# A hybrid convolution / state-space layer on one core: low weight parts from adding transfers, queues and products reassigned

## The chip, the core and the metric

The kernel runs on one core of a Trainium2 chip. Five engines work side by side, each through its own instructions in order: TensorE (PE: matrix products), VectorE (DVE), ScalarE (ACT), GpSimd (POOL) and SyncE (SP). They meet through semaphores. The scratch memory has 128 partitions; matrix products end in PSUM. The metric is the device time of one execution in microseconds, the median of several.

## The reference

One layer over 512 latent tokens (width 1024) with a context of 256 tokens ahead of them, in float32. Cut to what matters:

```python
h  = modulate(rmsnorm(x, norm1_w), mod[0], mod[1])       # hc likewise, from ctx
proj = h @ w_in                                          # columns: x, B, C, dt, z, glu, gate
glu = proj[..., COL_GLU:COL_GATE]
u = glu[..., :CONV_DIM] * sigmoid(glu[..., CONV_DIM:])
u = dwconv(u, conv_dw_w, conv_dw_b)                      # 31 taps along rows of 64
u_conv = silu(layernorm(u)) @ w_conv_out + b_conv_out
xs, bm, cm, dt_f, dt_b = ssd_inputs(proj, lp)            # 5 taps and SiLU on x, B, C
y_f, _ = ssd_scan(xs, dt_f, a[0], bm, cm, h_f)           # chunks of 128, both directions,
y_b, _ = ssd_scan(flip(xs), flip(dt_b), a[1], flip(bm), flip(cm), h_b)   # from context states
y = y_f + flip(y_b) + ssd_d * xs
u_ssd = rmsnorm(y * silu(z), ssm_norm_w) @ w_ssm_out
x = x + mod[2] * ((g_conv * u_conv + g_ssd * u_ssd) @ w_o)   # g: sigmoid of the gate columns
x = x + mod[5] * sq_relu_mlp(modulate(rmsnorm(x, norm2_w), mod[3], mod[4]), w_mlp1, w_mlp2)
out = rmsnorm(x, final_norm_w)
```

There are 8 groups of 4 heads; each has its own B and C (128 columns each), two tiles of x (X0, X1) and two of z (Z0, Z1).

## The kernel before

All activations lie transposed: a tile is 128 channels by 512 tokens. A matrix product in nearly full float32 is made from halves: a value v is split into a high part that TensorE takes (`whi`, `hh`) and a low part, the rest (`wlo`, `hl`). `gemm` runs, for each of 8 slices k of the 1024 inputs, high·high (L118), high·low (L119) and low·high (L120), 24 matmuls into one PSUM tile `ps`; 24 more of 256 columns follow where the context is needed (B, X0, X1).

`load_w` brings one weight of 128 output columns: SP starts the transfer of 512 KB into `raw` (L100, three buffers), ACT casts it to `whi` (L109), DVE subtracts, `wlo = raw - whi` (L110). `whi` and `wlo` have two buffers each, so the weight after next can be split only when the matmuls of a weight are through with its buffer.

Each group g has two stages. `proj(g)` runs B, C, X0, X1, Z0, Z1 through `gemm`; `taps5` evicts the PSUM tile on ACT with the middle tap (L377) and adds four taps on DVE straight from PSUM (L381), after which ACT applies SiLU (L391). `ssd(g)` makes the scan: C·B products `cps`, evicted to `cb`; transposes of B into `bps`, evicted by ACT to `Bk` (L485); transposes of X into `xps`; states `sps`; and for j = 0, 1 the output `yps`, with the decays. For these, rows that hold one head's values over time are broadcast from memory to all partitions: `E` rows (started by SP, L459; masked by POOL's affine_select, L463; exponentials on ACT, L466), and `Cd` rows (started by SP, L537; multiplied by C, L538: three of four on POOL, that of direction 0 and r = 1 on DVE). `yt` is then scaled and gated on DVE, stored to `s_y` by SP (L560), squared on ACT (L565) and added to `yacc` on POOL.

Behind the groups 0 to 4 a GLU tile is run: two more weights through `gemm` and 31 taps on DVE (`conv`, L593), the result added to `cacc` on POOL (L598). Three GLU tiles, the gates, the two branch projections, `w_o` and the MLP follow; there, too, `load_w` and `gemm` run all weights.

The program is written stage after stage, but a scheduler sets the order on each engine by priorities: `later(n)` moves what stands in it n places later (or earlier, if negative). Weights are asked for 300 places early, evictions 400. So matmuls of `proj(g + 1)` stand between those of `ssd(g)`, and an engine's row of instructions mixes both.

Of the kernel before, what the change touches and what calls it, by code (L numbers as in the profile page):

```python
# [8 lines left out]
F32 = mybir.dt.float32  # L9
F32R = mybir.dt.float32r  # L10
BF16 = mybir.dt.bfloat16
AF = mybir.ActivationFunctionType
ALU = mybir.AluOpType

P = 128
D = 1024
KT = 8
T = 512
# [32 lines left out]

WARM = 22

DECAYS_V = ((0, 1),)

W_EARLY, EVICT, EVICT_GLU, EVICT_FIRST = 300, 400, 200, 0
GLU_LATER, TAPS_LATER, LATE_LATER = 90, 650, 300
DT_LATER, LN_LATER, ROWS_LATER, BEGIN_LATER = 200, 100, 60, 60
# [2 lines left out]
def build(tc, xT, ctxT, cond, crow, wada1, wada2, vecs, hv, cst, w_in, w_co, w_so, w_o, w_1, w_2, outT):  # L61
    nc = tc.nc
    with ExitStack() as es:
# [26 lines left out]
        @contextmanager  # L90
        def later(n):

            tc.cur_priority += n
            yield
            tc.cur_priority -= n


        def load_raw(src):
            raw = wp.tile([P, KT, P], F32, name="raw", tag="raw", bufs=3)
            nc.sync.dma_start(raw, src)  # L100
            return raw

        def load_w(src, hi=None, lo=None, early=W_EARLY):
            with later(-early):
                raw = load_raw(src)
                if hi is None:
                    hi = wp.tile([P, KT, P], F32R, name="whi", tag="whi")
                    lo = wp.tile([P, KT, P], F32R, name="wlo", tag="wlo")
                nc.scalar.copy(hi, raw)  # L109
                nc.vector.tensor_tensor(lo, raw, hi, ALU.subtract)  # L110
            return hi, lo

        def gemm(ps, w, rhs, start=True, stop=True, t0=0, t1=None, k0=0, k1=KT):
            whi, wlo = w
            rhi, rlo = rhs
            ps = ps[:, t0:t1]
            for k in range(k0, k1):
                nc.tensor.matmul(ps, lhsT=whi[:, k, :], rhs=rhi[:, k, t0:t1], start=start and k == 0, stop=False)  # L118
                nc.tensor.matmul(ps, lhsT=whi[:, k, :], rhs=rlo[:, k, t0:t1], start=False, stop=False)  # L119
                nc.tensor.matmul(ps, lhsT=wlo[:, k, :], rhs=rhi[:, k, t0:t1], start=False, stop=stop and k == KT - 1)  # L120

        psum_pools = [pp]
        turn = [0]

# [72 lines left out]
        with tc.tile_pool(name="st", bufs=1) as st:  # L197
# [43 lines left out]
            for i in range(4):  # L241
# [12 lines left out]
                ps = pm.tile([P, T], F32, name="aps", tag="pm")  # L254
                for k in range(KT):
                    for j in range(4):
                        nc.tensor.matmul(
                            ps[32 * j:32 * j + 32, 0:P], lhsT=sc[:, k, :], rhs=blk[:, k, j * P:(j + 1) * P],
                            start=k == 0, stop=k == KT - 1)
# [35 lines left out]
        s_y = dr.tile([2 * KT, P, T], F32, name="s_y")  # L295
# [73 lines left out]
        spool = inner.enter_context(tc.tile_pool(name="sp", bufs=2))  # L369
# [49 lines left out]
        yacc = acct("yacc")  # L419
# [3 lines left out]
        never = nc.gpsimd.to_reg(NEVER)  # L423

        def proj(g):
            s = W_GRP + 6 * g
            if g == 0:
                _, Bt, Ct, X = first_xbc
            else:
                Bt = xbc(s, 16 + g, True, "Bt")  # L430
                Ct = xbc(s + 1, 24 + g, False, "Ct")
                X = [xbc(s + 2 + j, 2 * g + j, True, "Xt") for j in range(2)]
            Z = []
            for j in range(2):
                w = load_w(w_in[s + 4 + j], early=W_EARLY if g else 0)
                ps = ps_big()
                gemm(ps, w, rh)
                z = tp.tile([P, T], F32, name="Z", tag="Z", bufs=2)
                with later(-EVICT):
                    nc.scalar.activation(z, ps, AF.Silu)  # L440
                Z.append(z)
            return Bt, Ct, X, Z
# [28 lines left out]
        def ssd(g, Bt, Ct, X, Z):  # L471
# [19 lines left out]
            for c0 in (4, 0, 2):  # L491
# [10 lines left out]
                for d in range(2):  # L502
                    lo = c0 + 1 if (d == 1 and c0 == 0) else c0
                    hi = c0 + 1 if (d == 0 and c0 == 2) else c0 + 2
# [17 lines left out]
            for s in range(NCH - 1):  # L522
                ps = states(((s,), (3 - s,)))
# [6 lines left out]
            for j in range(2):  # L530
                yps = py.tile([P, T], F32, name="yps", tag="py")
                Ms, Cs = [], ([], [])
                for r in range(2):
                    for d in range(2):
                        hd = d * HEADS + 4 * g + 2 * j + r
                        Cd = (spool if d else tp).tile([P, T], F32, name="Cd", tag="Cd", bufs=CDB if d else 3)
                        nc.sync.dma_start(Cd, s_cf[hd, 1].unsqueeze(0).broadcast_to([P, T]))  # L537
                        (nc.vector if (d, r) in DECAYS_V else nc.gpsimd).tensor_tensor(Cd, Ct, Cd, ALU.mult)  # L538
                        Cs[d].append(Cd)
                    M = ahead.pop(0)  # L540
                    nc.vector.tensor_tensor(M, M, cb, ALU.mult)
                    Ms.append(M)
                expo(4 * g + 2 * j + 2 + LEAD)
                for k in range(3):
                    for c in range(NCH):
                        for r in range(2):
                            o = yps[64 * r:64 * r + 64, c * P:(c + 1) * P]
                            hr = 2 * j + r
                            if k == 2:
                                nc.tensor.matmul(o, lhsT=xt[:, c, hr, :], rhs=ch(Ms[r], c),  # L550
                                                 start=False, stop=True, skip_group_check=True)
# [5 lines left out]
                yt = tp.tile([P, T], F32, name="yt", tag="yt", bufs=2)  # L557
                nc.vector.scalar_tensor_tensor(yt, X[j][:, :T], vcol(V_D + t), yps, ALU.mult, ALU.add)
                nc.vector.tensor_tensor(yt, yt, Z[j], ALU.mult)
                nc.sync.dma_start(s_y[t], yt)  # L560
                if t == 0:
                    nc.scalar.activation(yacc, yt, AF.Square)
                else:
                    q = spool.tile([P, T], F32, name="ysq", tag="ysq", bufs=1)
                    nc.scalar.activation(q, yt, AF.Square)  # L565
                    nc.gpsimd.tensor_tensor(yacc, yacc, q, ALU.add)


# [35 lines left out]
        for g in range(G):  # L604
# [3 lines left out]
            if g in GLU_AT:  # L608
                with later(GLU_LATER):
                    q = glu(GLU_AT.index(g), spool, "sg")  # L610
                with later(TAPS_LATER):
                    taps(*q)
        late = list(range(len(GLU_AT), KT))
        inner.close()
        b2 = es.enter_context(tc.tile_pool(name="b2", bufs=5))
        p2 = es.enter_context(tc.tile_pool(name="p2", bufs=4, space=bass.MemoryType.PSUM))
# [278 lines left out]
```

## Time and profile before

| | |
|---|---|
| time, median of 3 runs | 1246.62 us (1246.41 to 1251.65) |
| profiled execution | 1245.49 us, its span 1243.7 us |
| granted TensorE clock, mean | 0.991 |
| busy: PE / DVE / ACT / POOL | 1203.5 / 922.5 / 549.8 / 167.7 us |
| transfers | 169.83 MB, mean 137 GB/s |

In the span the groups with their GLU tiles lie at about 110 to 503 us, some 70 us each, groups 6 and 7 to about 600, the late GLU tiles, gates and projections to about 900, the MLP behind them. The page's waits name an instruction that waited, the engine and line that released it, and the idle time. Matmuls overlap: a busy time of 0.39 us at a distance of 0.23 from start to start is full pace, and a gap is seen in the distance of starts.

### The profile page before, as it was taken

The page shows a single profiled execution, that of the slowest core. Times are in us where ns is not written, and L with a number is a line of the kernel's source. Part 1 is how long each engine was busy: PE and PEld are TensorE (multiplying, and loading weights), DVE is VectorE, ACT ScalarE, POOL GpSimd, SP SyncE. Part 2 cuts the span into 40 slices and gives each one's busy share as a digit, 9 for nine tenths or more (in the row PEclk, how much of TensorE's full clock was granted, in tenths as well). Part 3 has the DMA queues.
Part 4 walks back from the last instruction along what each step waited for, and adds up shares of the span by engine and source line. Part 5 has one row for each costly group of instructions (what it writes and reads, how often), then busy time and mean ns, then how long its engine had stood idle before and what let it go on. Part 6 is the DMA issues. An engine that isn't in the chain of part 4 may idle for free.

```text
span 1243.7 us, 17422 instructions
## 1 busy us (share of the span) xinstructions
PE 1203.5 (97%) x6662; PEld 995.1 (80%) x6662; DVE 922.5 (74%) x1426; ACT 549.8 (44%) x904; POOL 167.7 (13%) x138
## 2 busy tenths in 40 slices
PE   7999999999999999999999999999999999999997
PEld 3787888787777787787888788789988888888886
DVE  6799799898998989776999698777733343443454
ACT  4557976454554446342453461234422332322342
POOL 0004623141332423120010000000000000000000
PEclk7999999999999999999999999999999999999998
DMA  9427762533534352422353468855112332333322
GB/s 368 158 62 209 232 203 85 153 103 111 161 107 165 110 161 77 136 70 92 121 185 116 130 195 289 311 164 183 35 48 88 102 95 91 103 92 95 102 85 68
DMA packets 65331, 169.83 MB, mean 137 GB/s; under 512 B 7648, under 2 KB 10464, under 8 KB 65120
## 3 DMA queue, kind: packets, MB, share of 16 engines
q1 hardware_dynamic: 65248, 168.72, 42.6%
q8 instruction: 52, 0.85, 0.3%
q14 instruction: 31, 0.25, 0.1%
HBM read 162.14 MB, written 6.55 MB: 136 GB/s over the span
## 4 chain that ended last, share of the span: by engine, by line
PE 60%; DVE 19%; DMA 9%; ACT 6%; issue 3%; SPq 1%; POOL 1%; DVEq 0%; ACTq 0%; POOLq 0%
PE ps L118 18%; PE ps L120 18%; PE ps L119 18%; DVE conv L593 5%; DMA E<-s_cf 4%; DVE wlo L110 3%; DVE Xt L381 3%; ACT E L466 2%; PE sps L515 2%; DMA aw<-in_wada_dram 2%; DMA Cd<-s_cf 1%; PE yps L554 1%; ACT whi L109 1%; DVE Ct L381 1%; DVE Cd L538 1%
## 5 line engine op out<-in xcount | busy, mean ns | idle before, releaser
L109 ACT CAST whi<-raw 128x1024 fp32r<-128x1024 f32 x163 | 170.9, 1049 | 360.5 <-PE ps L119 329.0
L110 DVE TENSOR_TENSOR wlo<-raw,whi 128x1024 fp32r<-128x1024 f32 x163 | 202.3, 1241 | 94.7 <-ACT whi L109 86.6
L118 PE MATMUL ps<-hh,whi 128*128 128x512 f32 x632 | 255.7, 405 | 5.1 <-DVE Xt L381 2.4
L120 PE MATMUL ps<-hh,wlo 128*128 128x512 f32 x632 | 254.5, 403 | 5.5 <-DVE wlo L110 5.5
L119 PE MATMUL ps<-hl,whi 128*128 128x512 f32 x632 | 253.5, 401 | 0.0
L593 DVE SCALAR_TENSOR_TENSOR conv<-sg,V,conv 128x392 f32<-128x392 f32 (+14 forms) x240 | 181.6, 774 | 1.7
L120 PEld LDWEIGHTS ps<-hh,wlo 128*128 128x128 f32 x632 | 118.9, 188 | 35.2 <-DVE wlo L110 9.5
L118 PEld LDWEIGHTS ps<-hh,whi 128*128 128x128 f32 x632 | 118.8, 188 | 34.4 <-issue 9.7
L119 PEld LDWEIGHTS ps<-hl,whi 128*128 128x128 f32 x632 | 118.8, 188 | 24.8 <-issue 1.3
L730 DVE SCALAR_TENSOR_TENSOR x<-ps,mod,x 128x512 f32<-128x512 f32 (+1 forms) x48 | 31.6, 661 | 99.1 <-PE ps L120 99.1
L466 ACT ACTIVATE E<-E,bT 128x128 f32<-128x128 f32 x256 | 79.7, 394 | 38.9 <-POOL E L463 38.8
L120 PE MATMUL ps<-h2h,wlo 128*128 128x512 f32 (+1 forms) x240 | 89.9, 376 | 0.0
L119 PE MATMUL ps<-h2l,whi 128*128 128x512 f32 (+1 forms) x240 | 89.7, 375 | 0.0
L118 PE MATMUL ps<-h2h,whi 128*128 128x512 f32 (+1 forms) x240 | 89.7, 376 | 0.0
L119 PE MATMUL ps<-gl,whi 128*128 128x512 f32 x224 | 88.4, 395 | 0.0
L118 PE MATMUL ps<-gh,whi 128*128 128x512 f32 x224 | 88.2, 394 | 0.0
L120 PE MATMUL ps<-gh,wlo 128*128 128x512 f32 x224 | 87.9, 392 | 0.0
L538 POOL TENSOR_TENSOR Cd<-Ct,Cd 128x512 f32<-128x512 f32 x48 | 77.0, 1636 | 64.7 <-ACT Ct L391 56.1
L463 POOL TENSOR_SCALAR_AFFINE_SELECT E<-E 128x512 f32<-128x512 f32 x64 | 55.4, 878 | 207.7 <-DMA E<-s_cf 188.8
L381 DVE SCALAR_TENSOR_TENSOR Xt<-ps,V,Xt 128x510 f32<-128x510 f32 (+3 forms) x128 | 74.9, 607 | 2.6 <-ACT Xt L377 2.1
L118 PE MATMUL ps<-hc,whi 128*128 128x256 f32 x184 | 52.2, 284 | 1.4 <-DVE Xt L381 1.4
L119 PE MATMUL ps<-hc,whi 128*128 128x256 f32 x184 | 52.3, 284 | 0.0
(260 smaller groups left out, 2286.4 us busy)
## 6 DMA issues: line engine op xcount, KB each, us to landing
raw<-in_w_in_dram SPq DMA_DIRECT2D x81, 512.0 KB, 3.6
raw<-in_w_dram SPq DMA_DIRECT2D x64, 512.0 KB, 3.7
E<-s_cf SPq DMA_DIRECT2D x64, 256.0 KB, 4.6
Cd<-s_cf SPq DMA_DIRECT2D x64, 256.0 KB, 5.1
aw<-in_wada_dram SPq DMA_DIRECT2D x64, 256.0 KB, 4.3
ablk<-in_wada_dram SPq DMA_DIRECT2D x16, 512.0 KB, 8.3
raw<-in_w_so_dram SPq DMA_DIRECT2D x16, 512.0 KB, 3.7
s_y<-yt SPq DMA_DIRECT2D x16, 256.0 KB, 3.2
```

Of the source, the lines that this page charges most:

```text
L109: nc.scalar.copy(hi, raw)
L110: nc.vector.tensor_tensor(lo, raw, hi, ALU.subtract)
L118: nc.tensor.matmul(ps, lhsT=whi[:, k, :], rhs=rhi[:, k, t0:t1], start=start and k == 0, stop=False)
L119: nc.tensor.matmul(ps, lhsT=whi[:, k, :], rhs=rlo[:, k, t0:t1], start=False, stop=False)
L120: nc.tensor.matmul(ps, lhsT=wlo[:, k, :], rhs=rhi[:, k, t0:t1], start=False, stop=stop and k == KT - 1)
L381: nc.vector.scalar_tensor_tensor(o[:, lo:hi], ps[:, lo + d:hi + d], vcol(V_SCW + 5 * ch + j), o[:, lo:hi], ALU.mult, ALU.add)
L463: nc.gpsimd.affine_select(x3, x3, pattern=[[0, NCH], [sign, P]], compare_op=ALU.is_ge, fill=never, base=0, channel_multiplier=-sign)
L466: nc.scalar.activation(x3[:, c], x3[:, c], AF.Exp, bias=bT[:, c, hd:hd + 1])
L515: nc.tensor.matmul(ps[:, d * 256:(d + 1) * 256], lhsT=ch(Bk, c), rhs=xw[d][:, wi[d](c)].rearrange("p h e -> p (h e)"), start=i == 0, stop= ...
L538: (nc.vector if (d, r) in DECAYS_V else nc.gpsimd).tensor_tensor(Cd, Ct, Cd, ALU.mult)
L593: nc.vector.scalar_tensor_tensor(o[:, :, lo:hi], u[:, :, lo + d:hi + d], wv(j), o[:, :, lo:hi], ALU.mult, ALU.add)
L730: nc.vector.scalar_tensor_tensor(x1[:, j, a:b], ps[:, a:b], mod[:, gcol + j, 0:1], x1[:, j, a:b], ALU.mult, ALU.add)
```

## The change

From `proj(2)` on, until the pools of the groups are closed, `by_dma` is set: for the 36 weights of `proj(2)` to `proj(7)` and the 8 of the GLU tiles behind groups 1 to 4. There ACT starts the transfer of `raw` in place of SP. ACT casts `whi` as before and then writes `-raw` into `wlo`, which in that tile's type is minus the high part; POOL then starts a transfer of the same 512 KB from memory that adds to `wlo`, so that the low part is left. DVE subtracts nothing for these weights. All 64 products of C's rows are made by DVE. The square of `yt` goes to ACT first and the store to `s_y` is started by ACT behind it, so that SP starts only rows there. In the whole kernel `gemm` runs, where it covers all eight slices, the 16 matmuls with `whi` first and the 8 with `wlo` behind them.

```diff
-DECAYS_V = ((0, 1),)
-
         def load_raw(src):
             raw = wp.tile([P, KT, P], F32, name="raw", tag="raw", bufs=3)
-            nc.sync.dma_start(raw, src)
+            (nc.scalar if by_dma[0] else nc.sync).dma_start(raw, src)
             return raw
 
         def load_w(src, hi=None, lo=None, early=W_EARLY):
+            kept = hi is not None
             with later(-early):
...
                 nc.scalar.copy(hi, raw)
-                nc.vector.tensor_tensor(lo, raw, hi, ALU.subtract)
+                if kept or not by_dma[0]:
+                    nc.vector.tensor_tensor(lo, raw, hi, ALU.subtract)
+                else:
+
+                    nc.scalar.activation(lo, raw, AF.Copy, scale=-1.0)
+                    nc.gpsimd.dma_start(lo, src, accum_op=ALU.add)
             return hi, lo
 
         def gemm(ps, w, rhs, start=True, stop=True, t0=0, t1=None, k0=0, k1=KT):
...
+            whole = k0 == 0 and k1 == KT
+
+            def with_lo(k):
+                nc.tensor.matmul(ps, lhsT=wlo[:, k, :], rhs=rhi[:, k, t0:t1], start=False, stop=stop and k == KT - 1)
+
             for k in range(k0, k1):
                 nc.tensor.matmul(ps, lhsT=whi[:, k, :], rhs=rhi[:, k, t0:t1], start=start and k == 0, stop=False)
                 nc.tensor.matmul(ps, lhsT=whi[:, k, :], rhs=rlo[:, k, t0:t1], start=False, stop=False)
-                nc.tensor.matmul(ps, lhsT=wlo[:, k, :], rhs=rhi[:, k, t0:t1], start=False, stop=stop and k == KT - 1)
-
+                if not whole:
+                    with_lo(k)
+            if whole:
+                for k in range(KT):
+                    with_lo(k)
...
         def proj(g):
+            by_dma[0] = g > 1
...
                         nc.sync.dma_start(Cd, s_cf[hd, 1].unsqueeze(0).broadcast_to([P, T]))
-                        (nc.vector if (d, r) in DECAYS_V else nc.gpsimd).tensor_tensor(Cd, Ct, Cd, ALU.mult)
+                        nc.vector.tensor_tensor(Cd, Ct, Cd, ALU.mult)
...
-                nc.sync.dma_start(s_y[t], yt)
-                if t == 0:
-                    nc.scalar.activation(yacc, yt, AF.Square)
-                else:
-                    q = spool.tile([P, T], F32, name="ysq", tag="ysq", bufs=1)
-                    nc.scalar.activation(q, yt, AF.Square)
+                q = spool.tile([P, T], F32, name="ysq", tag="ysq", bufs=1) if t else yacc
+                nc.scalar.activation(q, yt, AF.Square)
+                nc.scalar.dma_start(s_y[t], yt)
+                if t:
                     nc.gpsimd.tensor_tensor(yacc, yacc, q, ALU.add)
...
         late = list(range(len(GLU_AT), KT))
+        by_dma[0] = False
         inner.close()
```

How this moves instructions is shown at three places of `proj(3)` and `ssd(2)`. Line numbers differ: the evictions L377 stand on L391 in the changed kernel, the exponentials L466 on L481, the masks L463 on L478, Bk L485 on L500, cacc L598 on L611, the cast L109 on L108; L98 is the start of a raw weight, L113 the negated copy, L114 the adding transfer.

ACT around X0's weight, before: `Bt` is B's eviction (512 columns of latents, 256 of context), `E` the exponentials, `Ct` C's eviction.

```order
L377 ACTIVATE Bt_2426<-ps_2427,V_72 128x512
L466 ACTIVATE E_2982<-E_2982,bT_575 128x128 x2
L109 CAST whi_2528<-raw_2526 128x1024
L377 ACTIVATE Bt_2426<-ps_2457,V_72 128x256
L466 ACTIVATE E_2982<-E_2982,bT_575 128x128 x2
L466 ACTIVATE E_2997<-E_2997,bT_575 128x128 x4
L466 ACTIVATE E_3529<-E_3529,bT_575 128x128 x4
L466 ACTIVATE E_3536<-E_3536,bT_575 128x128 x4
L377 ACTIVATE Ct_2494<-ps_2495,V_72 128x512
```

The same place after the change:

```order
L391 ACTIVATE Bt_2435<-ps_2436,V_72 128x512
L481 ACTIVATE E_2998<-E_2998,bT_575 128x128 x3
L481 ACTIVATE E_3005<-E_3005,bT_575 128x128
L108 CAST whi_2538<-raw_2536 128x1024
L391 ACTIVATE Bt_2435<-ps_2466,V_72 128x256
L113 ACTIVATE wlo_2539<-raw_2536 128x1024
L481 ACTIVATE E_3005<-E_3005,bT_575 128x128
L98 DMA raw_2708<-in_w_in_dram 128x1024
L481 ACTIVATE E_3005<-E_3005,bT_575 128x128
L108 CAST whi_2607<-raw_2605 128x1024
L481 ACTIVATE E_3005<-E_3005,bT_575 128x128
L481 ACTIVATE E_3013<-E_3013,bT_575 128x128 x2
```

X0's negated copy stands behind the eviction of B's context part, a transfer of a later weight and X1's cast among the exponentials.

ACT at the start of the next scan, before: `cb` and `Bk` are the evictions that `ssd` begins with.

```order
L478 COPY cb_2830<-cps_2825 128x512
L466 ACT_TABLE_LOAD
L466 ACTIVATE E_3551<-E_3551,bT_575 128x128
L485 COPY Bk_2832<-bps_2833 128x512
L485 COPY Bk_2832<-bps_2839 128x256
```

And after it:

```order
L493 COPY cb_2846<-cps_2841 128x512
L98 DMA raw_3167<-in_w_in_dram 128x1024
L500 COPY Bk_2848<-bps_2849 128x512
L500 COPY Bk_2848<-bps_2855 128x256
L481 ACT_TABLE_LOAD
L481 ACTIVATE E_3020<-E_3020,bT_575 128x128
```

The table load and the exponential went behind the two copies, and the start of a transfer came ahead of them.

POOL over the same stretch, before: the products of C (`Cd`), the masks of rows (`E`) and the two adds.

```order
L538 TENSOR_TENSOR Cd_2978<-Ct_2494,Cd_2978 128x512
L463 AFFINE_SELECT E_3551<-E_3551 128x512
L463 AFFINE_SELECT E_3612<-E_3612 128x512
L463 AFFINE_SELECT E_3627<-E_3627 128x512
L598 TENSOR_TENSOR cacc_585<-cacc_585,conv_720 128x512
```

And after it, from X0's weight on:

```order
L478 AFFINE_SELECT E_3553<-E_3553 128x512
L478 AFFINE_SELECT E_3560<-E_3560 128x512
L114 DMA wlo_2539<-in_w_in_dram 128x1024
L114 DMA wlo_2608<-in_w_in_dram 128x1024
L478 AFFINE_SELECT E_3575<-E_3575 128x512
L114 DMA wlo_2677<-in_w_in_dram 128x1024
L114 DMA wlo_2711<-in_w_in_dram 128x1024
L114 DMA wlo_2745<-in_w_in_dram 128x1024
L611 TENSOR_TENSOR cacc_585<-cacc_585,conv_720 128x512
L114 DMA wlo_2779<-in_w_in_dram 128x1024
```

Where the products of C were, POOL starts the adding transfers of X0, X1, Z0, Z1 and of the GLU tile's two weights, the last behind the add to `cacc`.

More of the change, by code (lines that the diff above doesn't have):

```diff
@@ L119, in gemm @@
                 nc.tensor.matmul(ps, lhsT=whi[:, k, :], rhs=rlo[:, k, t0:t1], start=False, stop=False)
-                nc.tensor.matmul(ps, lhsT=wlo[:, k, :], rhs=rhi[:, k, t0:t1], start=False, stop=stop and k == KT - 1)
+                if not whole:
[3 more added lines that the diff above has]
+                    with_lo(k)
+        by_dma = [False]
         psum_pools = [pp]
```

## The prediction, made before the changed kernel was run

> **What bounds the kernel now.** I read the page's busy times first, then windows cut at the group periods, then PE's waits inside them, then the timelines around each wait.
>
> ```profile
> PE 1203.5 (97%) x6662; PEld 995.1 (80%) x6662; DVE 922.5 (74%) x1426; ACT 549.8 (44%) x904; POOL 167.7 (13%) x138
> 293.30:364.20 70.90, 67.39 (x407) 55.73 (x408) 65.79 (x94) 34.12 (x66) 22.15 (x18) 1.00 0.42 129
> 950.00:1000.00 50.00, 50.00 (x221) 41.11 (x220) 20.51 (x23) 15.68 (x20) 0.00 (x0) 1.00 0.32 95
> ```
>
> A window row gives start:end and length, then busy time of PE, PEld, DVE, ACT and POOL, clock, DMA share, GB/s. PE is the bound: in 950:1000 it never rests, and 50.00 / 221 = 0.226 us is the pace of a 512-column matmul. The clock is full, so only gaps between matmuls can be won. In a period of a group with a GLU tile (such as 293.3:364.2) DVE is nearly as full as PE, and there the gaps lie:
>
> ```profile
> PE ps L120 <- DVE wlo L110: 5.1, 7, 0.7
> PE yps L554 <- DVE Cd L538: 3.3, 5, 0.9
> PE ps L118 <- DVE Xt L381: 2.4, 4, 0.7
> PE xps L495 <- ACT Bk L485: 1.5, 4, 0.4
> PE ps L118 <- DVE Bt L381: 0.4, 2, 0.2
> ```
>
> These are PE's waits in 222.7:560.7 (us in all, times, longest). One of them in PE's timeline (start, us, at the end the idle time):
>
> ```profile
> 327.93 0.40 PE L119 MATMUL ps<-hl,whi 128*128 128x512 f32 x1
> 329.05 0.50 PE L120 MATMUL ps<-hh,wlo 128*128 128x512 f32 x1 [0.73 <-DVE wlo L110]
> 329.39 0.40 PE L118 MATMUL ps<-hh,whi 128*128 128x512 f32 x1
> 329.63 0.39 PE L119 MATMUL ps<-hl,whi 128*128 128x512 f32 x1
> ```
>
> From 327.93 to 329.63 stand three steps, 0.68 us at the pace; they took 1.70. The wait shown as 0.73 cost 1.0, so a stall costs its idle time and some 0.27 us. The low part was late in DVE's queue, behind taps:
>
> ```profile
> 326.34 1.53 DVE L381 SCALAR_TENSOR_TENSOR Bt<-ps,V,Bt 128x254 f32<-128x254 f32 x3 [0.40 <-ACT Bt L377]
> 327.79 1.21 DVE L110 TENSOR_TENSOR wlo<-raw,whi 128x1024 fp32r<-128x1024 f32 x1
> ```
>
> **What is won.** The subtract leaves DVE for 44 weights: the 36 of proj(2) to proj(7) and the 8 of four GLU tiles. With 0.27 for each wait: low parts 5.1 + 7×0.27 = 7.0; Xt (a PSUM buffer that DVE's taps release late) 2.4 + 4×0.27 = 3.5; Bt 0.4 + 2×0.27 = 0.9. Bk is late on ACT:
>
> ```profile
> 361.38 1.28 ACT L466 ACT_TABLE_LOAD   x1 [1.05 <-DMA E<-s_cf]
> 363.22 0.40 ACT L466 ACTIVATE E<-E,bT 128x128 f32<-128x128 f32 x1 [0.56 <-POOL E L463]
> 363.53 0.84 ACT L485 COPY Bk<-bps 128x512 f32<-128x512 f32 x2
> ```
>
> It stands behind a table load and an exponential that waits for a row. In the changed order both copies of Bk come ahead of these, so 1.5 + 4×0.27 = 2.6 goes too. Sum 14.0.
>
> DVE has room for it:
>
> ```profile
> L110 DVE TENSOR_TENSOR wlo<-raw,whi 128x1024 fp32r<-128x1024 f32 x32 | 40.3, 1261 | 1.2 <-ACT whi L109 1.1
> L538 DVE TENSOR_TENSOR Cd<-Ct,Cd x16: 684/693/1741, 110.2 to 572.7; 128x512 f32<-128x512 f32 x16
> L538 POOL TENSOR_TENSOR Cd<-Ct,Cd x48: 1268/1694/2295, 109.3 to 543.2; 128x512 f32<-128x512 f32 x48
> ```
>
> The first row is of 222.7:503.4, the others give shortest/median/longest of the program. A period loses 8×1.26 = 10.1 us of subtracts and gets 6×0.69 = 4.1 of products: 65.8 becomes about 60. On POOL the same product takes 1.69 us, and the longest on DVE (1.74 against 0.68) shows that the two slow each other. So the Cd wait (3.3 + 5×0.27 = 4.7) shrinks by its multiplication, but a row that lands late stays: between 0 and 4.7 I take 1.5. In proj(1) and earlier DVE gets the products and keeps the subtracts, 12×0.69 = 8.3 us more in 100:222 for groups 0 and 1, of which a second subtract's worth may reach PE: I take a loss of 1, bounds −1 and 4.
>
> The new order in gemm needs the low part only after 16 high matmuls, 16×0.226 = 3.6 us later. For weights that keep the subtract, in 600:900:
>
> ```profile
> PE ps L120 <- DVE wlo L110: 1.3, 3, 0.7
> ```
>
> 1.3 + 3×0.27 = 2.1, all within 3.6 us; I take 2. Gains: 14.0 + 1.5 + 2 = 17.5, bounds 9 (half of the 14, and 2) and 21.
>
> **What it costs.** The low part now goes through ACT, POOL and the DMA queues. PE's end of the gemm two weights before frees the buffer, ACT writes −raw (1.05 us as the cast of the same size), POOL issues, and the sum must have landed when the 16 high matmuls of its own gemm are through. For X0 the buffer is free when the gemm of B's context part ends; before X0's low part come C's gemm (24×0.226 = 5.4) and 16 high matmuls (3.6), 9.0 in all. ACT uses of it the copy (1.05), the eviction ahead of it (0.56, first row below) and what of X0's cast and an exponential falls behind the gemm's end (I take 1.2): 6.2 us are left from POOL's issue to landing. Z1 has the same 9.0, without the 1.2: 7.4. The others have a context gemm more in between. POOL has two affine_selects ahead of X0's transfer, whose rows come earlier than now (below), and the add to cacc, which waits for the taps, ahead of that of the GLU tile's second weight, with some 7 us to spare by the same count. No accumulating transfer is in the trace; its neighbours are
>
> ```profile
> 325.75 0.56 ACT L377 ACTIVATE Bt<-ps,V 128x256 f32<-128x256 f32 x1
> L109 ACT CAST whi<-raw 128x1024 fp32r<-128x1024 f32 x163 | 170.9, 1049 | 360.5 <-PE ps L119 329.0
> raw<-in_w_in_dram SPq DMA_DIRECT2D x81, 512.0 KB, 3.6
> ablk<-in_wada_dram SPq DMA_DIRECT2D x16, 512.0 KB, 8.3
> L463 POOL TENSOR_SCALAR_AFFINE_SELECT E<-E 128x512 f32<-128x512 f32 x64 | 55.4, 878 | 207.7 <-DMA E<-s_cf 188.8
> GB/s 368 158 62 209 232 203 85 153 103 111 161 107 165 110 161 77 136 70 92 121 185 116 130 195 289 311 164 183 35 48 88 102 95 91 103 92 95 102 85 68
> ```
>
> Below, 3.6 as the plain load of the size; above, 8.3 as the transfer of the size in the crowded start. I take 6: 3.6, a second read of the 512 KB (1.4 at the 368 GB/s of the page's first slice), and POOL's own work, by affine_select's mean some 0.9. At 6 X0 is just in time: 1 us over the six groups. Bounds: 0 at 3.6, and at 8.3 (2.1 + 0.27 + 0.9 + 0.27)×6 = 21. [...]
>
> ACT gets per GLU period 8 copies (8×1.05 = 8.4), 10 DMA issues and 4 more table loads (2 become 6):
>
> ```profile
> 332.03 1.28 ACT L391 ACT_TABLE_LOAD   x1
> 318.10 0.32 SPq L560 DMA_DIRECT2D s_y<-yt  x1
> ```
>
> 4×1.28 = 5.1, 10×0.32 = 3.2: 34.1 becomes 51 of 70. It is covered as long as ACT has 19 us of rest. But ACT works in order, and behind these stand the evictions of B, C and X, whose taps release PSUM, and Bk. If one of the table loads stands ahead of an eviction once a period and 0.7 of it reaches PE, that is 0.7×6 = 4. Bounds 0 and two whole loads a period, 15.
>
> SP now only carries rows. An E row stood behind the store (issued at 318.10, once yt was there), and its exponential held ACT 4.30 us:
>
> ```profile
> 324.21 0.69 ACT L466 ACTIVATE E<-E,bT 128x128 f32<-128x128 f32 x2 [4.30 <-POOL E L463]
> Cd<-s_cf SPq DMA_DIRECT2D x64, 256.0 KB, 5.1
> ```
>
> That becomes earlier. Against it, 8 more transfers of 512 KB a period: 4.2 MB on 9.1 (129 GB/s × 70.9 us), and C's rows, already 5.1 us to landing, may land some 0.5 later ahead of the second yps: 0.5×6 = 3, bounds 0 and 10 (a third of the landing time more, 1.7 a group). [...]
>
> Sum: 17.5 − 1 − 1 − 4 − 3 = 8.5. The profiled execution took 1245.49 (span 1243.7 and 1.8 around it), so 1237.0 for a profiled one; the median of the runs shown, 1246.62, lies 1.1 above it, and I forecast 1238.
>
> **The rivals.**
> (A, late sums: slower.) The accumulating transfer is what PE waits on. It decides from about 7.4 us, where X0 is late by 1.2 + 0.27 and 6×1.5 = 9 eats what is won; at 8.3 it gives 1238 + 21 − 1 = 1258, at 9.5 (X0 3.3 + 0.27, Z1 2.1 + 0.27 a group, 5.9×6 = 36) 1273. For it: the 8.3 of ablk, and that each sum needs three engines in turn. Against it: DMA share is only 0.42 there. 0.17.
> (B, held issue: slower or same.) [...] 0.08.
> (C, the stalls change hands: same.) Evictions behind ACT's table loads, or C's rows, take what DVE gave back: losses of 10 to 17, so 1239 to 1247, middle 1244. For it: ACT at 73% in order, with 14 more table loads in all. Against it: DVE's queue was the fuller one by far. 0.22.
> (D, everything covered.) Nothing but the gains: 1246.6 − 17.5 = 1229. 0.10.
>
> **How the numbers follow.** The forecast's case has 0.43, its own range 1231 to 1243. Of the median, 0.5% is 6.2 us, about what a measurement of this kernel can tell from no change: faster ends at 1240.4, slower begins at 1252.9. Faster: 0.36 of the forecast's case, D's 0.10, 0.06 of C: 0.52. Slower: 0.15 of A, 0.05 of B, 0.02 of C: 0.22. Same: 0.26. The range runs from D's time to A's at 8.3, a microsecond beyond each: 1228 to 1259.
>
> **What would show it.** Right: the subtract's waits at the low part gone between 222 and 560, Xt and Bk waits gone, DVE near 60 of a shorter period, the accumulating transfer at 5 to 7 us from issue to landing, PE's gaps down from 14 to about 6 us. Wrong: low-part matmuls waiting on a DMA (A; B, if POOL's issue itself is long), or the same sum of gaps with ACT evictions or C's rows named (C).

## The result, and the profile after

The changed kernel took 1268.86 us (median of 4 runs, 1264.78 to 1274.56) against 1248.68 of the kernel before beside it; the ratio is 1.0167 with a 95% interval of 1.0145 to 1.0189. It is slower, where faster was forecast, and lies beyond the range. The profiled span went from 1243.7 to 1267.3 us.

The page of the changed kernel first: busy times, and the queues of transfers (q0 is POOL's, q10 ACT's, q1 SP's; the numbers are packets, MB and the time of their packets as a share of the 16 engines' span).

```profile
PE 1210.9 (96%) x6662; PEld 1006.3 (79%) x6662; DVE 880.5 (69%) x1430; ACT 619.4 (49%) x962; POOL 120.0 (9%) x134
...
q1 hardware_dynamic: 56608, 141.45, 35.2%
q0 software_dynamic: 6336, 23.07, 10.1%
q10 hardware_dynamic: 8640, 27.27, 7.2%
...
raw<-in_w_in_dram ACTq DMA_DIRECT2D x44, 512.0 KB, 5.2
wlo<-in_w_in_dram POOLq DMA_DIRECT2D x44, 512.0 KB, 7.3
...
E<-s_cf SPq DMA_DIRECT2D x64, 256.0 KB, 5.3
Cd<-s_cf SPq DMA_DIRECT2D x64, 256.0 KB, 5.9
```

DVE's busy time fell by 42 us and PE's grew by 7, with the same number of matmuls. A packet of the adding transfer took 0.101 × 1267.3 × 16 / 6336 = 0.323 us of one engine; the raw weights and the stores on ACT's queue took 0.169. An adding transfer needed 7.3 us to land in the median, where 6 was assumed, and the other transfers were slower beside it: raw weights 5.2 for 3.6, C's rows 5.9 for 5.1.

PE's waits in the same stretch as before the change, 222.7:560.7:

```profile
PE yps L569 <- DVE Cd L553: 10.2, 5, 2.6
PE ps L124 <- DMA wlo<-in_w_in_dram: 7.1, 4, 2.6
PE ps L127 <- DVE Bt L395: 5.0, 3, 2.6
```

The waits on the subtract, on the taps of Xt and on Bk are gone. In their place stand twelve, most of them far longer than any before: on the products of C's rows, on low parts that land late, and on the taps of B. Two periods of the changed kernel, from one yps wait to the next (start:end and length, busy time of PE, PEld, DVE, ACT, POOL, granted clock, DMA share, GB/s), and under them the first of them in the kernel before:

```profile
250.41:324.70 74.29, 69.44 (x406) 59.02 (x407) 59.97 (x96) 52.27 (x93) 18.16 (x21) 0.95 0.76 184
324.70:400.34 75.64, 68.08 (x407) 57.09 (x407) 56.67 (x92) 47.58 (x77) 16.77 (x19) 0.98 0.68 175
```

```profile
241.63:312.14 70.51, 67.28 (x406) 55.76 (x407) 66.00 (x94) 34.06 (x65) 21.77 (x17) 1.00 0.40 127
```

DVE's load fell as forecast (66 to 57 or 60) and ACT's rose as forecast (34 to 48 or 52). The DMA share went from 0.40 to about 0.72, though the bytes only from 127 to 180 GB/s. And the clock, 1.00 before, is 0.95 and 0.98. One wait with what follows, in windows of the changed kernel:

```profile
248.00:250.00 2.00, 0.00 (x0) 0.00 (x0) 0.34 (x1) 0.00 (x0) 0.00 (x0) 1.00 1.03 345
250.00:251.00 1.00, 0.59 (x10) 0.59 (x12) 1.00 (x3) 0.01 (x1) 0.00 (x0) 1.00 1.08 268
251.00:252.00 1.00, 1.00 (x16) 1.00 (x14) 1.00 (x2) 1.00 (x3) 0.29 (x1) 0.57 1.07 250
252.00:253.00 1.00, 1.00 (x12) 1.00 (x10) 0.96 (x2) 0.79 (x3) 1.00 (x1) 0.50 1.02 250
...
254.00:255.00 1.00, 1.00 (x11) 0.83 (x8) 0.38 (x2) 0.00 (x0) 0.00 (x0) 0.73 1.04 387
```

PE stands still up to 250.4, and behind the wait the clock is at half for 3.4 us. From the trace's record of the clock, this happens seven times between 100 and 640 us in the changed kernel, six times for 3.41 us and once for 6.83, 27.3 us in all: up to 13.7 us lost. In the kernel before there is no such stretch between 30 and 1234 us.

So the account of the 23.6 us of span: PE starts its last yps matmul 20.6 us later (595.75 for 575.16), and 3 us more are lost behind it, where the changed kernel waits 2.6 us for `mh` and 1.4 for a cast. For the 20.6 us there are two things in 100:640. Distances between matmuls that are over 0.25 us too long, against the pace of 0.226 us, add up to 34.1 us of excess, against 23.4 before (+10.7); and the half clock adds up to 13.7. Together that is 4 us more than the 20.6: the two overlap in places and shorter gaps are left out, which was not taken apart.

### The profile page after: what moved, and what is told of

Read it like the earlier page. It is cut to its first block, busy times and chain, and to the rows that moved or that the text cites. A ratio compares the mean times of both kernels' runs of the same rounds, so it can differ in the third digit from the quotient of the medians.

```text
span 1267.3 us, 17431 instructions
## 1 busy us (share of the span) xinstructions
PE 1210.9 (96%) x6662; PEld 1006.3 (79%) x6662; DVE 880.5 (69%) x1430; ACT 619.4 (49%) x962; POOL 120.0 (9%) x134
## 3 DMA queue, kind: packets, MB, share of 16 engines
q0 software_dynamic: 6336, 23.07, 10.1%
## 4 chain that ended last, share of the span: by engine, by line
PE 78%; DMA 11%; DVE 6%; issue 2%; ACT 2%; SPq 1%; POOL 0%; DVEq 0%; POOLq 0%; ACTq 0%
PE ps L124 23%; PE ps L127 23%; PE ps L128 23%; DMA Cd<-s_cf 3%; DMA aw<-in_wada_dram 3%; DMA wlo<-in_w_in_dram 3%; PE sps L530 3%; PE yps L569 2%; DVE wlo L110 1%; DVE aw L708 1%; DMA E<-s_cf 1%; PE xps L510 1%; PE yps L565 1%; DMA s_dec<-dec 1%; DMA x_sb<-in_xT_dram 1%
## 5 line engine op out<-in xcount | busy, mean ns | idle before, releaser
L108 ACT CAST whi<-raw 128x1024 fp32r<-128x1024 f32 x163 | 171.3, 1051 | 284.3 <-PE ps L128 264.8
L110 DVE TENSOR_TENSOR wlo<-raw,whi 128x1024 fp32r<-128x1024 f32 x119 | 145.8, 1226 | 177.9 <-ACT whi L108 101.2
L606 DVE SCALAR_TENSOR_TENSOR conv<-sg,V,conv 128x464 f32<-128x464 f32 (+14 forms) x240 | 170.3, 726 | 6.5 <-ACT conv L600 4.2
L124 PE MATMUL ps<-hh,wlo 128*128 128x512 f32 x632 | 163.0, 396 | 7.5 <-DMA wlo<-in_w_in_dram 7.5
L481 ACT ACTIVATE E<-E,bT 128x128 f32<-128x128 f32 x256 | 83.1, 394 | 32.9 <-POOL E L478 31.9
L395 DVE SCALAR_TENSOR_TENSOR Xt<-ps,V,Xt 128x255 f32<-128x255 f32 (+3 forms) x128 | 73.0, 608 | 5.1 <-ACT Xt L391 4.6
L478 POOL TENSOR_SCALAR_AFFINE_SELECT E<-E 128x512 f32<-128x512 f32 x64 | 49.3, 781 | 210.4 <-DMA E<-s_cf 196.9
L553 DVE TENSOR_TENSOR Cd<-Ct,Cd 128x512 f32<-128x512 f32 x64 | 42.3, 685 | 20.6 <-DMA Cd<-s_cf 19.9
L124 PE MATMUL ps<-h2h,wlo 128*128 128x512 f32 (+1 forms) x240 | 56.4, 376 | 0.0
L124 PE MATMUL ps<-gh,wlo 128*128 128x512 f32 x224 | 55.4, 389 | 0.0
L114 POOL DMA_DIRECT2D wlo<-in_w_in_dram x44 | 38.3, 872 | 179.5 <-ACT wlo L113 166.5
L569 PE MATMUL yps<-Cd,hst 128*64 128x128 f32 x512 | 40.4, 300 | 13.5 <-DVE Cd L553 13.5
L127 PEld LDWEIGHTS ps<-h2h,whi 128*128 128x128 f32 x240 | 44.8, 188 | 8.3 <-ACT h2h L788 0.2
```

The source lines that it names most:

```text
L114: nc.gpsimd.dma_start(lo, src, accum_op=ALU.add)
L395: nc.vector.scalar_tensor_tensor(o[:, lo:hi], ps[:, lo + d:hi + d], vcol(V_SCW + 5 * ch + j), o[:, lo:hi], ALU.mult, ALU.add)
L478: nc.gpsimd.affine_select(x3, x3, pattern=[[0, NCH], [sign, P]], compare_op=ALU.is_ge, fill=never, base=0, channel_multiplier=-sign)
L481: nc.scalar.activation(x3[:, c], x3[:, c], AF.Exp, bias=bT[:, c, hd:hd + 1])
L553: nc.vector.tensor_tensor(Cd, Ct, Cd, ALU.mult)
L569: nc.tensor.matmul(o, lhsT=hst[:, s, k, hr * 64:hr * 64 + 64], rhs=ch(Cs[k][r], c), start=k == 0 and c == 0, stop=False, skip_group_check= ...
```

## The experiments

Ratios are to the kernel before, run beside it on the same chip, with 95% intervals. "Lost at waits" below is the excess of over-long distances between matmuls, as above, in 100:640 of the profiled execution, "half clock" the length of such stretches there.

### Without the adding transfers

The low parts are subtracted on DVE again; everything else is as in the change.

```diff
-                if kept or not by_dma[0]:
+                if True:
                     nc.vector.tensor_tensor(lo, raw, hi, ALU.subtract)
```

> The changed kernel with the low parts made by DVE's subtract again, in all weights; the raw weights and the stores still started by ACT, the products of C on DVE, the new order of matmuls. Theory L: DMA share in the groups falls from 0.73 to about 0.45, rows land in about 5 us, PE's waits at yps fall under 1 us apiece and no half clock follows: 1243 to 1250. Theory Q: the waits at yps stay at 2 us and more, since SP's order and DVE's queue are as in the change, and DVE has 10 us a period more to do: 1258 to 1268.

1236.92 us, ratio 0.9931 (0.9906 to 0.9955). The remaining edits make the kernel faster, and the adding transfers with what belongs to them (ACT's copies, POOL's starts) turned that into a loss: by the ratios 0.0236, some 29 us between the two (the medians differ by 32, but the kernel before beside them differed too). Lost at waits 9.1 us (34.1 with the adding), half clock 6.8 (27.3). C's rows land in 5.1 us. That is theory L, and faster than it said, though one yps wait of 1.9 us with a half clock behind it is left.

### A plain transfer in place of the adding one

POOL brings the same bytes without adding: the subtraction is left out of this kernel.

```diff
-                    nc.gpsimd.dma_start(lo, src, accum_op=ALU.add)
+                    nc.gpsimd.dma_start(lo, src)
```

> The changed kernel with a plain transfer in place of the adding one: POOL brings the same 512 KB into the low part without adding, so the subtraction is left out; instructions, queues and order stay. Measures what the adding itself costs: the profile of the change shows 10.1% of the queues' span for 23.07 MB by POOL's queue against 7.2% for 27.27 MB by ACT's, about 1.7 times per byte. Theory L: landing falls from 7.3 to about 5.5 us, the waits at the low part go, the time falls to 1250 to 1258. Theory Q: the waits on C's rows and their half clock stay, and the time falls by the low part's waits alone, 7.5 us and their half clock, to about 1258 to 1264.

1246.55 us, ratio 1.0008 (0.9988 to 1.0028). Its queue and landing:

```profile
q0 software_dynamic: 6336, 23.07, 5.4%
...
wlo<-in_w_in_dram POOLq DMA_DIRECT2D x44, 512.0 KB, 4.7
```

The same packets without the addition take 0.054 × 1245 × 16 / 6336 = 0.170 us, half of 0.323, and land in 4.7 us instead of 7.3. So the 29 us split into some 20 for the addition itself (1.0167 against 1.0008) and some 10 for carrying the weights twice, with ACT's copies and less the subtract (1.0008 against 0.9931). The low part's waits all but went (0.7 us once), but the rows of C stayed late: PE's waits in 100:640 are here

```profile
PE yps L569 <- DVE Cd L553: 9.3, 7, 2.3
```

Half clock fell from 27.3 us to 6.8, though several of these waits are nearly as long (2.3 us at most); the last section has waits of that length without half clock in the changed kernel, too.

### The products of C's rows on DVE, alone

```diff
-                        (nc.vector if (d, r) in DECAYS_V else nc.gpsimd).tensor_tensor(Cd, Ct, Cd, ALU.mult)
+                        nc.vector.tensor_tensor(Cd, Ct, Cd, ALU.mult)
```

> The kernel before with all products of C's rows on DVE, nothing else changed. Theory Q (queue heads: a product that waits for its row's transfer stands at the head of DVE's queue, and taps and other work behind it wait too): PE's waits on DVE grow, the yps waits to 2 us and more apiece, long waits are followed by stretches at half the clock, the time is 1255 to 1262. Theory L (load: the 44 adding transfers fill the DMA queues, and rows land late because of them): without them rows land as before (5.1 us), and the time is within 4 us of before, since DVE only gets 33 us of products and loses contention with POOL.

1233.27 us, ratio 0.990 (0.9864 to 0.9937). Neither theory had expected a gain: this edit is worth 12 us by itself. Its period from one yps wait to the next, and its waits in 222.7:560.7:

```profile
242.53:309.95 67.42, 66.23 (x405) 55.89 (x405) 66.64 (x100) 34.41 (x65) 11.26 (x11) 1.00 0.43 130
```

```profile
PE ps L118 <- DVE Bt L381: 1.5, 1, 1.5
PE yps L554 <- DVE Cd L538: 1.5, 4, 0.5
PE ps L118 <- DVE Ct L381: 0.6, 1, 0.6
```

DVE runs six products more in the period and is busy 66.6 us, as before (66.0). So the work that it had before got shorter by about as much as the products cost on DVE, 6×0.68 = 4.1 us. Rows of 225:503 show where, of the kernel before and of this one:

```profile
L593 DVE SCALAR_TENSOR_TENSOR conv<-sg,V,conv 128x392 f32<-128x392 f32 (+14 forms) x118 | 98.2, 833 | 1.0
L538 DVE TENSOR_TENSOR Cd<-Ct,Cd 128x512 f32<-128x512 f32 x8 | 8.5, 1059 | 2.5 <-DMA Cd<-s_cf 2.5
```

```profile
L593 DVE SCALAR_TENSOR_TENSOR conv<-sg,V,conv 128x424 f32<-128x424 f32 (+14 forms) x120 | 90.4, 753 | 0.8
L538 DVE TENSOR_TENSOR Cd<-Ct,Cd 128x512 f32<-128x512 f32 x32 | 21.7, 678 | 0.7 <-DMA Cd<-s_cf 0.5
```

A tap takes 753 ns in the mean for 833, a product 678 for 1059. The median tap is nearly the same, 688 ns for 701: what went is slow ones, 30 of 118 taps over 0.95 us before and 11 of 120 here (10 of 117 in the changed kernel, where DVE has the products, too). In the trace of before all 30 ran beside an instruction of POOL, 12 of them beside a product; the 75 taps with none beside them took 0.68 us in the mean and 0.74 at most. That it was the products that slowed them is likely, but not shown apart. The waits on the subtract went without the subtract being touched. Which part of that comes from faster instructions and which from the order that the scheduler made anew, no run here separates.

### The products back on POOL, in the changed kernel

```diff
-                        nc.vector.tensor_tensor(Cd, Ct, Cd, ALU.mult)
+                        (nc.vector if (d, r) == (0, 1) else nc.gpsimd).tensor_tensor(Cd, Ct, Cd, ALU.mult)
```

> The changed kernel with three of four products of C's rows on POOL again. The products on DVE alone gave 12 us; if that gain is also in the change, this is slower by 8 to 14, 1277 to 1283. If with the subtracts gone DVE has room enough that the slowing of each other no longer matters, within 4 us of the change. If POOL's products delay the starts of the adding transfers, more than 14 slower.

1287.5 us, ratio 1.0344 (1.0323 to 1.0364): 18 thousandths above the change, some 22 us. The gain of the products was in the change, and more than alone: POOL, which starts the adding transfers in its order, now also waits for C there (20.1 us idle ahead of its products). In 100:640 the waits are

```profile
PE ps L124 <- DMA wlo<-in_w_in_dram: 19.3, 12, 3.3
PE yps L569 <- DVE Cd L553: 16.3, 8, 3.3
```

against 7.5 and 13.5 us in the change. That is the third case of the expectation.

### The order of matmuls, alone

The edit of `gemm` as in the change, nothing else.

```diff
-                nc.tensor.matmul(ps, lhsT=wlo[:, k, :], rhs=rhi[:, k, t0:t1], start=False, stop=stop and k == KT - 1)
+                if not whole:
+                    with_lo(k)
+            if whole:
+                for k in range(KT):
+                    with_lo(k)
```

> The kernel before with the new order of matmuls in gemm alone (16 high ones, then 8 low ones, for whole weights). By my sum the ten waits of the low part on the subtract (6.4 us idle in the whole span before, some 9 us with 0.27 for each) are covered by 16 matmuls of 0.226 us, and nothing else moves: about 1238 to 1240. If the stall only moves on to the next thing that DVE owes PE (the PSUM buffer behind the taps of Xt and Bt), the time stays within 3 us of before.

1248.31 us, ratio 1.0021 (1.0 to 1.0041). The subtract's ten waits are gone and nothing is won. Lost at waits are 23.5 us, for 23.4: they stand elsewhere, in 100:640 at

```profile
PE yps L563 <- DVE Cd L547: 6.5, 8, 1.3
PE ps L123 <- DVE Xt L390: 4.7, 5, 1.2
```

And in 600:1000 a new one stands, with a half clock behind it at 832 us:

```profile
PE ps L123 <- ACT mh L140: 2.6, 1, 2.6
```

This is the start of `w_o`, whose right side comes slice by slice: with the low matmuls in between, PE had three matmuls to do for each slice, now two.

### The store of yt by ACT, alone

```diff
-                nc.sync.dma_start(s_y[t], yt)
...
+                nc.scalar.activation(q, yt, AF.Square)
+                nc.scalar.dma_start(s_y[t], yt)
```

> The kernel before with the store of yt started by ACT behind its square, nothing else. In the prediction a row stood behind the store on SP and an exponential waited 4.3 us for it: if that wait matters, some 1 to 3 us less, 1243 to 1245; if not, within 2 us of before; if the stores on ACT delay evictions, up to 1250.

1242.59 us, ratio 0.9984 (0.9969 to 0.9998): about 2 us less, between 0.2 and 3.9 by the interval. That fits the first case and the second alike: the store's place on SP mattered little.

### Raw weights by SP again, in the changed kernel

```diff
-            (nc.scalar if by_dma[0] else nc.sync).dma_start(raw, src)
+            nc.sync.dma_start(raw, src)
```

> The changed kernel with the raw weights started by SP again, adding transfers and all else as in the change. If ACT's ten starts and the order that they bring there hold the evictions up (rival C of the prediction), the time falls by 5 to 10 us, to about 1260. If SP's queue to itself is worth something to the rows, it rises to 1270 to 1280, since rows stand behind raw weights again. If neither, within 3 us of the change.

1271.58 us, ratio 1.0199 (1.0166 to 1.0232), beside 1.0167 (1.0145 to 1.0189) of the change. The intervals overlap: which engine starts the raw weights makes no difference that these runs tell. ACT's starts are not what made the change slow.

### C's weight alone subtracted, in the changed kernel

In the changed kernel the second yps of a group waits for C's rows. SP's and POOL's timelines around it (start, us), and DVE's product:

```profile
244.43 1.27 SPq L552 DMA_DIRECT2D Cd<-s_cf  x3
```

```profile
244.83 0.87 POOL L114 DMA_DIRECT2D wlo<-in_w_in_dram  x1
```

```profile
249.66 0.69 DVE L553 TENSOR_TENSOR Cd<-Ct,Cd 128x512 f32<-128x512 f32 x1 [2.69 <-DMA Cd<-s_cf]
```

The rows are asked for at 244.4 to 245.7, when the first yps has released their buffers, and 0.4 us behind the first of them POOL starts the adding transfer for C's weight, just behind a raw weight of ACT (244.51). The windows above show the queues full there, DMA share 1.0 and more, and this adding transfer took 11.4 us to land. A switch brings back the subtract for some weights only:

```diff
-                if kept or not by_dma[0]:
+                if kept or not by_dma[0] or by_sub[0]:
...
+                by_sub[0] = "C" in SUB
                 Ct = xbc(s + 1, 24 + g, False, "Ct")
```

> The changed kernel in which C's weight of each group (six of the 44) is split by DVE's subtract again; the other 38 keep the adding transfer. In the change the adding transfer of C's weight is started 0.4 us behind the rows that the second yps waits for (POOL at 244.83, SP's rows from 244.43). Theory L1 (that one transfer, beside those rows, makes them late): the waits at yps fall from 2.5 us to under 1.5 us apiece and their half clock goes, some 4.4 us for each of five: time 1245 to 1253. Theory L2 (the load of all 44 together): one eighth of it less changes little, 1262 to 1268.

1257.26 us, ratio 1.0091 (1.0061 to 1.012). Of 44 adding transfers 38 are left, and 0.0076 of the ratio, some 9 us, is gone. In 222:560 the waits are

```profile
PE ps L126 <- DMA wlo<-in_w_in_dram: 10.5, 6, 4.0
PE ps L129 <- DVE Bt L398: 3.3, 4, 1.5
PE yps L579 <- DVE Cd L563: 3.0, 5, 1.0
```

The yps waits fell from 10.2 us, 2.6 at most, to 3.0, 1.0 at most, and no half clock stands behind them any more: the one transfer beside the rows made them late (L1). The whole gain is smaller than L1 said, since the low parts became later, 10.5 us for 7.1, and the 13.7 us of half clock that are left in the groups all stand at them. C's late subtract or the shorter wait ahead may be why; that was not taken apart.

### C, X0 and Z1 subtracted, in the changed kernel

The same with `SUB = ("C", "X0", "Z1")`, in X0 and Z1 likewise.

> The changed kernel with DVE's subtract for C, X0 and Z1 of each group (18 of the 44), the adding transfer for the other 26, those with more time. If the loss is the low parts that land late at X0 and the rows late at yps, both go, and DVE has 3.7 us a period more to do: 1235 to 1242, as without any adding. If it is the load of the queues, 26 of 44 keep 26/44 of the 32 us: 1250 to 1258.

1241.78 us, ratio 0.9972 (0.9955 to 0.9989). No wait on a low part is left between 100 and 640, though 26 adding transfers remain and land in 7.1 us. So 18 of the 44 carried 0.0195 of the ratio, some 24 of the 29 us, more than their share by number. Where they fell, C's beside the rows and X0's with the least time, explains that; in the change all five waits on a low part in 100:640 are X0's, none is Z1's. But no run takes another 18 away, so it isn't shown that only these would do. Still, 0.9972 is slower than 0.9931 without any adding: with no low part late, the adding transfers still gain nothing here over DVE's subtract of 1.2 us.

### Two that are faster: the products with and without the order

The new order together with all products on DVE:

> The kernel before with two edits: all products of C's rows on DVE, and the new order of matmuls. Alone the first gave 0.990 and the second 1.002. With the products on DVE four waits of the low part were left (3.6 us idle, some 4.7 us lost): if the order takes these, 1228 to 1230. If they move on to the PSUM buffers behind DVE's taps, as with the order alone, 1232 to 1238.

1236.92 us, ratio 0.9916 (0.9886 to 0.9946), no better than the products alone. A wait stands there that the change has too (3.8 us in it, with the half clock of 6.83 us). Its row among PE's waits in 100:640, and DVE's timeline ahead of it:

```profile
PE dtp L369 <- DVE conv L354: 2.3, 1, 2.3
```

```profile
109.19 0.69 DVE L547 TENSOR_TENSOR Cd<-Ct,Cd 128x512 f32<-128x512 f32 x1 [2.97 <-DMA Cd<-s_cf]
...
110.46 0.55 DVE L354 TENSOR_TENSOR conv<-conv 128x384 f32<-128x384 f32 x1
```

A product of group 0 stands at the head of DVE's queue, waits 2.97 us for its row, and behind it stands the last step (L354) of the time-step part, on which PE's transposes wait. It takes both edits: with the products alone this wait is 0.6 us, as before, and with the order alone it isn't in the list. So in group 0 the products are left on POOL:

```diff
-                        nc.vector.tensor_tensor(Cd, Ct, Cd, ALU.mult)
+                        (nc.vector if g or (d, r) in DECAYS_V else nc.gpsimd).tensor_tensor(Cd, Ct, Cd, ALU.mult)
```

> The new order of matmuls and the products on DVE from group 1 on; group 0 keeps three of four on POOL. With the products of group 0 on DVE a product that waits for its row stands ahead of the last step of the time-step part, on which the transposes into dtp wait: 2.4 us idle and a stretch of half clock there. If that is the cause, this wait falls to about 0.6, the half clock at 112 us goes, and the time falls by some 4 us against the version with all products on DVE (1236.9), to 1231 to 1234.

1231.66 us, ratio 0.9900 (0.988 to 0.992). The dtp wait is no more among PE's waits in 100:640, and there is no half clock there. The named wait is gone as expected. The time is not shown to have fallen: the medians differ by 5 us, the ratios by 0.0016, some 2 us, and the intervals overlap.

The same without the new order:

> The kernel before with the products on DVE from group 1 on, and nothing else. That all of them were on DVE gave 0.990 with no long wait at dtp; if group 0's products brought nothing there, 1231 to 1236; if relieving POOL in the crowded first group was part of the gain, 1236 to 1240.

1231.53 us, ratio 0.9899 (0.9882 to 0.9916). The order adds nothing to it, and leaving group 0 out makes no difference that these runs tell (0.990 with all products on DVE). One line of the kernel before, 12 to 13 us less.

## Why the prediction was wrong, point by point

The subtract's removal: right in what it named. The waits on the low part's subtract, on Xt's buffer and on Bk are gone from 222:560. Bt's are not: 5.0 us for 0.4. And the 14 us weren't DVE's subtract's to give alone. Moving the products off POOL took most of the same waits, with the subtract left in place. No run removes the subtract and nothing else.

The products (taken at 1.5, bounds 0 and 4.7): mis-sized, they gave 12 us alone. The row of DVE's longest product (1.74 us for 0.68) was quoted, but the slowing was priced at the products' own waits and not at DVE's other work, whose slow taps went when the products left POOL.

The loss of 1 us in groups 0 and 1: DVE's work was counted there, but not what an in-order product that waits for a row holds up behind it, in the order that came with the new gemm. It was the dtp wait: 3.8 us and a half clock of 6.83.

The order (taken at 2, for the late part): 1.0021 alone. It covered the subtract's waits as worked out and brought the 2.6 us at `w_o`, which the prediction left out: there a `gemm` starts on a right side that is still being made and loses one of three matmuls of cover.

What the adding transfers cost is the step that failed: 1 us for the low part, 3 for C's rows and 4 for evictions behind ACT, 8 in all, and nothing for a half clock. The run without them is some 29 us faster than the change. The next four points take these in turn.

The low part's time (1 us over six groups). X0's chain in the changed kernel, ACT first, then POOL, then PE:

```profile
261.82 1.48 ACT L481 ACTIVATE E<-E,bT 128x128 f32<-128x128 f32 x4
263.21 1.04 ACT L108 CAST whi<-raw 128x1024 fp32r<-128x1024 f32 x1
264.15 0.56 ACT L391 ACTIVATE Bt<-ps,V 128x256 f32<-128x256 f32 x1
264.61 1.05 ACT L113 ACTIVATE wlo<-raw 128x1024 fp32r<-128x1024 f32 x1
```

```profile
266.07 0.64 POOL L478 TENSOR_SCALAR_AFFINE_SELECT E<-E 128x512 f32<-128x512 f32 x1 [0.38 <-DMA E<-s_cf]
266.65 0.87 POOL L114 DMA_DIRECT2D wlo<-in_w_in_dram  x1
```

```profile
261.95 0.40 PE L127 MATMUL ps<-hh,whi 128*128 128x512 f32 x1
...
273.78 2.75 PE L124 MATMUL ps<-hh,wlo 128*128 128x512 f32 x8 [2.58 <-DMA wlo<-in_w_in_dram]
```

C's gemm starts at 261.95, which is when X0's buffer is free. ACT is through at 265.66, 3.7 us later where 2.8 was taken, since four exponentials stand ahead of the cast. POOL starts the transfer 1.0 us after that, behind a mask that waited for its row; nothing was taken for this. Landing takes about 7 us where 6 was taken. So 0.9 + 1.0 + 1.0, and a sum that was "just in time" was late by 2.6. In proj(3) to proj(6) X0's negated copy ended some 4 to 7 us after the buffer was free and the transfer landed in 6.1 to 8.5: ACT's order was the larger miss, not the landing.

C's rows (3 us, bounds 0 and 10) are the larger part: 13.5 us idle in 100:640 for 3.7 before, with half clock of 3.41 us behind four of the seven waits. With 0.27 for each wait and 1.7 for each of these stretches, an estimate from the rows above, they cost some 22 us, and the low parts, with one such stretch, some 11. The prediction spread the added bytes over the period; the trace and the two runs with C's weight show one transfer beside the rows that PE needs next.

Evictions behind ACT (4 us, bounds 0 and 15): Bt's three waits and one half clock make some 7.5 us by the same count. The table loads that the prediction feared were not what stood ahead:

```profile
337.20 0.41 ACT L481 ACTIVATE E<-E,bT 128x128 f32<-128x128 f32 x1 [2.47 <-POOL E L478]
337.51 0.76 ACT L391 ACTIVATE Bt<-ps,V 128x512 f32<-128x512 f32 x1
```

B's eviction stands on ACT behind an exponential that waits for POOL's mask, and for its PSUM buffer PE waits 2.63 us at 342.81. The wait of 1.81 us at 491.90 has the same ahead of it.

The half clock: in no term, though it cost up to 13.7 us, more than the waits grew. The forecast priced a wait at its idle time and 0.27 us, from waits of up to 0.9 us. The rows of before that could have warned are those of the first 30 us and the last 10, where waits of 3.6 and 1.9 us stand beside half clock.

Of the rivals, A named one of the two mechanisms: late sums. Its condition was 7.4 us, and 7.3 was measured; at that it had some 1246, since it held neither the half clock nor the rows. C was half right: the stalls did change hands, to C's rows and to evictions behind ACT, but it priced them at 10 to 17 us and put them down to table loads. The run with raw weights on SP speaks against ACT's starts. B's chance rests on an issue held up while DVE works, which no run shows: POOL's start of a transfer took 0.86 to 1.01 us each of the 44 times in the changed kernel.

## What to carry to other kernels

Before a subtraction is turned into an adding transfer, list for each of them when it can start and when it must have landed, and what else is on the queues in these microseconds: here 18 of 44 carried most of the loss. When work moves from one engine to another, count what both lose by working at the same time; here six products more a period left DVE's busy time as it was (66.6 us for 66.0). An instruction that waits for a transfer belongs on an engine with nothing urgent behind it: a product's 2.97 us on DVE here held up a step that TensorE then waited 2.3 us for. And a wait of some 2 us on TensorE should be priced with the 1.7 us that a half clock of 3.41 us behind it may cost.

## What the runs showed of the hardware

In these kernels an adding transfer took about twice the queue time of a plain one: 0.323 us against 0.170 us for the same packets of 4 KB or less, and 7.3 us against 4.7 us to land 512 KB.

The clock of TensorE fell to half behind single waits of 1.9 to 4 us (1.90 in the kernel without adding, 3.98 in the first microseconds of the changed kernel, ended at 12.16, half clock from 12.20). In the groups of the changed kernel it then stayed there for 3.41 us six times and for 6.83 once. It is not a matter of length alone: in the changed kernel a wait of 2.27 us (ended at 324.70) and one of 2.31 (350.60) had no half clock behind them, and in the kernel without adding one of 1.90 us had:

```profile
446.44 1.93 PE L569 MATMUL yps<-Cd,hst 128*64 128x128 f32 x18 [1.90 <-DVE Cd L553]
```

Windows there (start:end, length, busy time of PE, clock, DMA share, GB/s):

```profile
446.00:447.00 1.00, 0.56 (x8) 0.88 0.93 303
447.00:448.00 1.00, 1.00 (x14) 0.50 0.92 352
```

In the changed kernel it goes with where a wait falls. Its seven stretches in 100:640 start at 111.19, 182.87, 251.13, 275.03, 343.30, 401.32 and 473.00 us: neighbours lie 21, 20, 7, 20, 17 and 21 times 3.413 us apart, which is also the length of the short ones in the trace's record of the clock. Cut the time into cells of 3.413 us at these points and sum PE's idle time in each. The cells that end where the half clock starts have 2.17 to 2.63 us of it; the waits before 324.70 and 350.60 are each split over two cells, with 1.88 and 1.83 us in the fuller one. Between 100 and 1200 us each of the seven cells with 2.0 us of idle time or more has half clock behind it, and none of the five with 1.5 to 2.0 us. The second half of the stretch of 6.83 us doesn't fit: the cell before it has 1.16 us. In the kernel before no cell there has 1.5 us, and there is no half clock. The 1.90 us above, with half clock behind it, lies under 2.0 us as well, so no limit is shown by this.
